# Turning HGRN's normed and gated result with VectorE's square blocks and a trip through memory instead of 16 TensorE transposes

## The chip, the cores and the metric

The kernel runs on one core of a Trainium2 chip. The metric is the device time of one execution in microseconds (us). The kernel before takes 1633.6 us, the median of 3 runs (1633.28 to 1634.9).

The core has five engines, each with its own in-order queue: TensorE (PE in the profile, its weight loads PEld), VectorE (DVE), ScalarE (ACT), GpSimd (POOL) and SyncE (SP). Here SP issues the transfers of weights, and POOL the transfers of pages through memory.

## The reference, cut to what matters

One layer works on 256 latent and 256 context tokens of 2048 features, all in float32: a modulated norm, one wide input projection, a convolution branch and a bidirectional HGRN recurrence side by side, a gated merge with an output projection, and an MLP. The change lies between the recurrence and its output projection:

```python
def hgrn_readout(o, g, norm_g, w_o):
    o = rms_norm(o, norm_g.reshape(HGRN_HEADS, HGRN_HEAD_DIM))
    o = o.reshape(o.shape[:2] + (D_HGRN,)).astype(g.dtype) * jax.nn.silu(g)
    return o @ w_o
...
y_h = hgrn_readout(o, p_g, hgrn_norm_g[l], hgrn_out_w[l])
```

There are 8 heads of 128 features. For each token and head, `o` is divided by its root mean square over the 128 features, scaled by a gain per feature and by silu of a gate per token and feature; then all 1024 features are projected to 2048.

## The kernel before

**Products.** Every float32 product is made of two-part numbers: `hi` is the value rounded to TensorE's float32r, `lo` what is left. ScalarE makes `hi` of a weight tile (`whi`, L124), VectorE makes `lo` (`wlo`, L127). A token-wise product (`tokens`, L280, through `mm3r`, L259, and `pe`, L183 and L188) does, per weight tile of 128 x 1024, four output blocks of three matmuls each: 12 matmuls of 128 x 512. A product over 16 tiles does tiles 0 to 12 one after the other, and calls `pump` after each; tiles 13 to 15 are taken together, block by block (LAST = 3), and then its four sums are evacuated. Four tiles of `hi` and `lo` are held (AHEAD = 4), five raw tiles wait or are in flight (RAWS = 5).

**Order of the work.** The Tile framework plans each engine's order when the program is built, by program order and its own estimate of when an instruction could run; an instruction that is ready may be planned far ahead of where the program has it. `issue_after` holds an instruction behind another on the same engine. Work beside the products sits in generators on the list `bg`. `pump` (L161) gives them a budget of so many us per call (1.3 here, never more than 2.5), in the order of the list, the first three only (LIVE = 3). A generator yields its cost on VectorE, or None to wait for the next call. What it issues on VectorE is held behind the last but one `wlo` (L168), so that it can't pass the weights; nothing holds what it issues on the other engines. `finish` (L177) runs a generator to its end.

**Around the change.** After the recurrence, the order of the products is: the convolution's gate and value, silu(g) (L839, tokens on partitions, kept in `self.sg`), the two merge gates (L853 and L854, each in two halves of 16 weight tiles), the HGRN output projection (`who`, L863), the convolution's projection (`wpw`). The convolution and its layer norm (`conv`, L1540) are a generator from L829 on, and the two readouts (`readout`, L1517, four heads each) follow it on the list from L841 on. They run beside the two gates, and L857 finishes them ahead of the HGRN projection.

**The readout.** Head `h` has left `o` with tokens on partitions, 2 blocks of 128 tokens by 128 features, in a page of four heads (`self.on`), and its sums of squares in `self.osq`. The readout takes the reciprocal root (L1523), multiplies by it and by silu(g) (L1528, VectorE, in place, 2 per head), turns the two blocks to features on partitions with TensorE against the identity into a PSUM bank (L1533), and evacuates it twice, scaled by the norm's gain: to `hi` by ScalarE (L1536), to `lo` by VectorE (L1537). The two parts go to `self.rp[h]`, the operand of the projection, in memory that held the context's activations.

**Pages.** On-chip buffers of 128 x 1024 floats come from one pool of 30 pages (`page`, L194); each is given back after its last reader.

**The turn without TensorE.** The MLP turns its hidden values in another way. `turn_blocks` (L1246) transposes 32 x 32 blocks of 512 columns with one VectorE instruction (L1250). `swapped` (L1279) stores the page to memory (L1284) and loads it back in four transfers (L1287) that put the blocks' rows on their partitions. `turn_hidden` (L1252) waits ten calls of `pump` and then splits the page that came back (L1270 through L240), held on ScalarE behind the newest `whi`.

Of the kernel before, what the change touches and what calls it, by code (L numbers as in the profile page):

```python
# [8 lines left out]
F32 = mybir.dt.float32  # L9
# [3 lines left out]
AF = mybir.ActivationFunctionType  # L13
ALU = mybir.AluOpType

P = 128
T = 256
# [17 lines left out]
PB = 4  # L35
# [102 lines left out]
class Kernel:  # L138
# [1378 lines left out]
    def readout(self, j):  # L1517

        nc = self.nc
        while self.ended < 4 * (j + 1):  # L1520
            yield None
        r = self.osq[:, 8 * j:8 * j + 8]
        self.rstd(r, r, 1.0 / P)  # L1523
        for h in range(4 * j, 4 * j + 4):
            o = self.at(self.on, h)
            for tb in range(2):
                s = o[:, tb * P:(tb + 1) * P]
                nc.vector.scalar_tensor_tensor(s, s, self.osq[:, 2 * h + tb:2 * h + tb + 1], self.sg[tb][:, h * P:(h + 1) * P], op0=ALU.mult, op1=ALU.mult)  # L1528
            yield 0.5
            yield None  # L1530
            ps = self.bank()
            for tb in range(2):
                nc.tensor.transpose(out=ps[:, tb * P:(tb + 1) * P], in_=o[:, tb * P:(tb + 1) * P], identity=self.v["ident"])  # L1533
            g = self.v["hng"][:, h:h + 1]
            hi, lo = self.rp[h][:, :T], self.rp[h][:, T:]
            nc.scalar.activation(out=hi, in_=ps[:, :T], func=AF.Copy, scale=g)  # L1536
            nc.vector.scalar_tensor_tensor(lo, ps[:, :T], g, hi.bitcast(F32), op0=ALU.mult, op1=ALU.subtract)  # L1537
            yield 0.5

    def conv(self, uhv, uvv):  # L1540
# [153 lines left out]
```

## Time and profile before

| | |
|---|---|
| median of 3 runs | 1633.6 us (1633.28 to 1634.9) |
| profiled execution, first to last instruction (the page gives no other time of it) | 1632.6 us |
| TensorE busy | 1615.6 us, 99% |
| VectorE busy | 1162.2 us, 71% |
| ScalarE busy | 784.3 us, 48% |
| POOL busy | 52.0 us, 3% |
| TensorE's 16 turns at L1533 | 658.3 to 711.6 us |
| evacuations of the gates, L850 | 597.7 to 739.7 us |
| bytes moved | 391.22 MB, 240 GB/s in the mean |

In the rows of the profile, `L1533 PE MATMUL bank<-pack,o` is a line of the kernel, an engine, an operation, and the tile written with the tiles read. `x16` counts instructions. A bracket such as `[0.19 <-DVE o L1528]` is the time for which the engine sat idle just before, and the instruction that ended it. Matmuls are pipelined: they are shown with their latency and overlap each other.

### The profile page before, as it was taken

The numbers are of one execution on the slowest core, as the hardware profiler recorded it, in microseconds if no ns is written. First come the engines' busy times: TensorE is split into PE (matmuls) and PEld (weight loads), VectorE is DVE, ScalarE is ACT, GpSimd is POOL, SyncE is SP. The second block draws the span as 40 slices with busy tenths as digits, with TensorE's granted clock in tenths as the row PEclk, the third lists the DMA queues.
The fourth block names the chain that finished last, engine by engine and source line by source line (L and its number), as shares of the span: only waits on it lengthen the run. The fifth ranks groups of instructions, "written<-read, shape, count | busy, mean of one in ns | idle before, by whom it ended". The sixth has DMA issues, their size and how long they took to land.

```text
span 1632.6 us, 21510 instructions
## 1 busy us (share of the span) xinstructions
PE 1615.6 (99%) x7939; PEld 1337.5 (82%) x7939; DVE 1162.2 (71%) x1686; ACT 784.3 (48%) x1094; POOL 52.0 (3%) x98
## 2 busy tenths in 40 slices
PE   7999999999999999999999999999999999999998
PEld 5668888888888888888888888888888888888887
DVE  5786887778868889977887676545665656665556
ACT  6553444434554444654446665444553455435543
POOL 0000000000000000000000001000110011001000
PEclk9999999999999999999999999999999999999999
DMA  9997954444566566787887478867887688677763
GB/s 377 402 379 281 324 175 151 149 152 135 194 202 219 182 192 205 236 279 267 320 302 254 142 259 256 287 197 235 289 283 227 217 255 284 231 240 241 232 217 114
DMA packets 109145, 391.22 MB, mean 240 GB/s; under 512 B 12912, under 2 KB 13680, under 8 KB 109040
## 3 DMA queue, kind: packets, MB, share of 16 engines
q1 hardware_dynamic: 102096, 368.60, 66.4%
q0 software_dynamic: 6656, 20.99, 4.3%
q8 instruction: 62, 1.02, 0.3%
q14 instruction: 43, 0.35, 0.1%
q10 hardware_dynamic: 288, 0.26, 0.0%
HBM read 379.32 MB, written 10.49 MB: 239 GB/s over the span
## 4 chain that ended last, share of the span: by engine, by line
PE 94%; DVE 2%; DMA 1%; issue 1%; ACT 1%; SPq 0%; ACTq 0%; DVEq 0%
PE bank L188 82%; PE bank L255 5%; PE bank L257 3%; PE bank L1465 2%; DVE wlo L127 1%; DMA x<-ctx 1%; ACT whi L124 0%; DMA raw<-who 0%; PE bank L1496 0%; PE bank L1507 0%; PE bank L1505 0%; DMA raw<-wpw 0%; DVE gacc L1301 0%; SPq L526 0%; PE bank L1360 0%
## 5 line engine op out<-in xcount | busy, mean ns | idle before, releaser
L127 DVE TENSOR_TENSOR wlo<-raw,whi 128x1024 fp32r<-128x1024 f32 x488 | 593.0, 1222 | 321.2 <-ACT whi L124 315.1
L124 ACT ACTIVATE whi<-raw 128x1024 fp32r<-128x1024 f32 x488 | 512.9, 1059 | 605.2 <-PE bank L188 388.5
L188 PE MATMUL bank<-whi,h 128*128 128x512 f32 x2160 | 674.1, 390 | 2.0 <-DVE h L673 1.2
L188 PEld LDWEIGHTS bank<-whi,h 128*128 128x128 f32 x2160 | 405.1, 188 | 88.0 <-DVE h L673 2.1
L188 PE MATMUL bank<-wlo,h 128*128 128x512 f32 x1080 | 420.7, 390 | 1.3 <-DVE wlo L127 1.3
L188 PEld LDWEIGHTS bank<-wlo,h 128*128 128x128 f32 x1080 | 202.8, 188 | 44.9 <-DVE wlo L127 3.5
L188 PE MATMUL bank<-whi,hidh 128*128 128x512 f32 x503 | 195.0, 388 | 0.0
L188 PE MATMUL bank<-wlo,hidh 128*128 128x512 f32 x503 | 195.0, 388 | 0.0
L188 PE MATMUL bank<-whi,hidl 128*128 128x512 f32 x503 | 195.0, 388 | 0.0
L188 PE MATMUL bank<-h,whi 128*128 128x512 f32 x512 | 166.2, 405 | 0.0
L188 PEld LDWEIGHTS bank<-whi,hidl 128*128 128x128 f32 x503 | 94.4, 188 | 19.5
L188 PEld LDWEIGHTS bank<-wlo,hidh 128*128 128x128 f32 x503 | 94.4, 188 | 19.3
L188 PEld LDWEIGHTS bank<-whi,hidh 128*128 128x128 f32 x503 | 94.4, 188 | 19.3
L188 PEld LDWEIGHTS bank<-h,whi 128*128 128x128 f32 x512 | 91.3, 189 | 20.6 <-issue 6.2
L188 PE MATMUL bank<-h,wlo 128*128 128x512 f32 x256 | 100.0, 391 | 0.0
L255 PE MATMUL bank<-h,whi 128*128 128x512 f32 x384 | 97.8, 396 | 0.0
L255 PEld LDWEIGHTS bank<-h,whi 128*128 128x128 f32 x384 | 69.0, 189 | 12.4
L1314 DVE SCALAR_TENSOR_TENSOR raw<-raw,silu_row 128x1024 f32<-128x1024 f32 x64 | 76.6, 1219 | 0.4 <-DMA raw<-wmt 0.3
L1301 DVE SCALAR_TENSOR_TENSOR gacc<-raw,silu_c,gacc 128x1024 f32<-128x1024 f32 x60 | 76.7, 1278 | 0.0
L188 PEld LDWEIGHTS bank<-h,wlo 128*128 128x128 f32 x256 | 48.1, 188 | 10.2
L257 PEld LDWEIGHTS bank<-h,wlo 128*128 128x128 f32 x384 | 52.4, 190 | 3.9
L257 PE MATMUL bank<-h,wlo 128*128 128x256 f32 x384 | 53.5, 282 | 0.0
(246 smaller groups left out, 1374.5 us busy)
## 6 DMA issues: line engine op xcount, KB each, us to landing
raw<-w SPq DMA_DIRECT2D x256, 512.0 KB, 4.8
raw<-wi SPq DMA_DIRECT2D x172, 512.0 KB, 4.5
raw<-wmt SPq DMA_DIRECT2D x64, 512.0 KB, 4.3
raw<-wm SPq DMA_DIRECT2D x64, 512.0 KB, 4.8
rawpage<-wm SPq DMA_DIRECT2D x42, 512.0 KB, 9.7
raw<-wo SPq DMA_DIRECT2D x32, 512.0 KB, 4.8
raw<-who SPq DMA_DIRECT2D x16, 512.0 KB, 5.1
raw<-wpw SPq DMA_DIRECT2D x16, 512.0 KB, 5.6
```

What stands on the lines that cost most here:

```text
L124: kn.his.append(nc.scalar.activation(out=hi, in_=raw, func=AF.Copy))
L127: kn.los.append(nc.vector.tensor_tensor(lo, raw, hi.bitcast(F32), op=ALU.subtract))
L188: ins = fn(*args, **kw)
L255: nc.tensor.matmul(bank, w[0][:, cut(i)], x(k)[2], start=(k == 0), stop=False)
L257: nc.tensor.matmul(bank[:, T:], w[1][:, cut(i)], x(k)[0], start=False, stop=(k == nk - 1))
L1301: nc.vector.scalar_tensor_tensor(acc, raw, s, acc, op0=ALU.mult, op1=ALU.add)
L1314: nc.vector.scalar_tensor_tensor(raw, raw, 1.0, self.srow, op0=ALU.mult, op1=ALU.mult, accum_out=self.dot[:, 32 * j + b:32 * j + b + 1])
L1465: nc.tensor.matmul(ps[:, b * P:(b + 1) * P], w, r, start=True, stop=True)
```

## The change

The readout no longer uses TensorE or PSUM. L1528 stays, and the generator yields once for two heads. When the four heads of a readout are done, VectorE transposes 32 x 32 blocks of their page into a new page, `oflip`, with two instructions of 512 columns; the page is stored to memory and loaded back in four transfers by `swapped`, into another page; the generator passes eight calls of `pump`; then, for each head, ScalarE copies the head's columns out of the returned page into a small buffer (`gained`), putting the blocks in order and scaling by the norm's gain, and `split` makes `hi` (ScalarE) and `lo` (VectorE) of it.

```diff
@@ readout
                 nc.vector.scalar_tensor_tensor(s, s, self.osq[:, 2 * h + tb:2 * h + tb + 1], self.sg[tb][:, h * P:(h + 1) * P], op0=ALU.mult, op1=ALU.mult)
-            yield 0.5
+            if h % 2:
+                yield 0.5
+        flip = self.page(F32, "oflip")
+        for n in range(2):
+            self.turn_blocks(flip, n, self.on[j][:, n * 512:(n + 1) * 512])
+            yield 0.7
+        back = self.swapped(flip).rearrange("p (i b r) -> p b i r", i=4, b=8)
+        for _ in range(8):
             yield None
-            ps = self.bank()
-            for tb in range(2):
-                nc.tensor.transpose(out=ps[:, tb * P:(tb + 1) * P], in_=o[:, tb * P:(tb + 1) * P], identity=self.v["ident"])
-            g = self.v["hng"][:, h:h + 1]
-            hi, lo = self.rp[h][:, :T], self.rp[h][:, T:]
-            nc.scalar.activation(out=hi, in_=ps[:, :T], func=AF.Copy, scale=g)
-            nc.vector.scalar_tensor_tensor(lo, ps[:, :T], g, hi.bitcast(F32), op0=ALU.mult, op1=ALU.subtract)
+        for n in range(PB):
+            h = PB * j + n
+            g, src = self.v["hng"][:, h:h + 1], back[:, 2 * n:2 * n + 2]
+            t = self.small(T, "gained")
+            nc.scalar.activation(out=t.rearrange("p (b i r) -> p b i r", b=2, i=4), in_=src, func=AF.Copy, scale=g)
+            self.split(t, self.rp[h][:, :T], self.rp[h][:, T:])
             yield 0.5
```

The helpers that it calls, unchanged:

```python
def turn_blocks(self, page, j, src):
    out = page[:, :TW].rearrange("p (j b r) -> p b j r", j=4, b=8)[:, 4 * j:4 * j + 4]
    self.nc.vector.transpose(out=out, in_=src.rearrange("p (b j r) -> p b j r", b=4, j=4))

def swapped(self, page):
    there = self.dr.tile([P, TW], F32, name="there", tag="there", bufs=4)
    nc.gpsimd.dma_start(there, page[:, :TW])
    back = self.page(F32, "back")[:, :TW]
    for j in range(4):
        nc.gpsimd.dma_start(back[32 * j:32 * j + 32].rearrange("c (i f) -> c i f", i=4),
                            there[:, j * T:(j + 1) * T].rearrange("(i c) f -> c i f", i=4))
    return back
```

## The prediction

> **What bounds the kernel now.** I read the page's first part, then the stretch in which the readouts run, then the chain of waits inside it.
>
> ```profile
> span 1632.6 us, 21510 instructions
> PE 1615.6 (99%) x7939; PEld 1337.5 (82%) x7939; DVE 1162.2 (71%) x1686; ACT 784.3 (48%) x1094; POOL 52.0 (3%) x98
> ```
>
> TensorE is busy for 99% of the span, so a turn taken off it can shorten the kernel by what the turn takes there, and by no more. The 16 turns, and the products that feed them, run between 658 and 712 us (here the instructions that touch the tile `o`, with minimum, median and maximum ns):
>
> ```profile
> L1528 DVE SCALAR_TENSOR_TENSOR o<-o,osq,silu_g x16: 339/347/352, 657.9 to 710.1; 128x128 f32<-128x128 f32 x16
> L1533 PEld LDWEIGHTS bank<-pack,o x16: 137/139/143, 658.3 to 711.5; 128*128 128x128 f32 x16
> L1533 PE MATMUL bank<-pack,o x16: 270/272/329, 658.3 to 711.6; 128*128 128x128 f32 x16
> ```
>
> Busy time by stretch; after the stretch come its length, then PE, PEld, DVE, ACT and POOL busy with counts, the clock, the DMA share and GB/s:
>
> ```profile
> 655.00:690.00 35.00, 34.81 (x157) 27.94 (x156) 35.00 (x52) 20.48 (x26) 0.00 (x0) 1.00 0.70 229
> 700.00:740.00 40.00, 40.00 (x180) 33.09 (x179) 27.33 (x34) 20.64 (x29) 1.20 (x2) 1.00 0.79 269
> ```
>
> VectorE is busy for all of 655 to 690 us: there two engines are full at once, since the convolution's layer norm runs beside the readouts. From 700 to 740 VectorE has a third to spare.
>
> **The turns on TensorE.** 272 ns is a latency; what a turn keeps from the next product is read from TensorE's order in time (start, us, engine, line, operation):
>
> ```profile
> 657.52 0.39 PE L188 MATMUL bank<-wlo,h 128*128 128x512 f32 x1
> 657.75 0.39 PE L188 MATMUL bank<-whi,h 128*128 128x512 f32 x1
> 658.33 1.12 PE L1533 MATMUL bank<-pack,o 128*128 128x128 f32 x4 [0.19 <-DVE o L1528]
> 659.20 0.48 PE L188 MATMUL bank<-whi,h 128*128 128x512 f32 x1
> 659.52 0.40 PE L188 MATMUL bank<-wlo,h 128*128 128x512 f32 x1
> ```
>
> And the chain of waits in the same run, where a pair of turns is followed by products alone:
>
> ```profile
> 681.04 0.22 PE bank L1533 x2
> 681.26 24.72 PE bank L188 x108
> ```
>
> A product takes 24.72 / 108 = 0.229 us, three of them 0.69. From one `wlo` product to the next, with the first four turns between, 2.00 us pass: 1.31 more, 0.4 of it the wait for L1528. Each of the six later pairs stands in the chain with 0.22 us. The sum is 1.31 + 6 x 0.22 = 2.6 us. [...]
>
> **What VectorE and ScalarE gain and lose.** The evacuations L1536 and L1537 go. What comes has rows of its like: the split at L240 of the same shape, and the MLP's block turn L1250 (same helper, same shape). Instructions that write or read `h`, on ScalarE and then on VectorE, and the block turn:
>
> ```profile
> L1536 ACT ACTIVATE h<-bank,pack x8: 452/458/479, 659.2 to 712.7; 128x256 fp32r<-128x256 f32 x8
> L240 ACT ACTIVATE h<-conv x8: 400/402/419, 699.1 to 708.0; 128x256 fp32r<-128x256 f32 x8
> ```
>
> ```profile
> L1537 DVE SCALAR_TENSOR_TENSOR h<-bank,pack,h x8: 390/476/482, 661.5 to 713.8; 128x256 fp32r<-128x256 f32 x8
> L240 DVE TENSOR_TENSOR h<-conv,h x8: 415/418/424, 700.1 to 709.1; 128x256 fp32r<-128x256 f32 x8
> ```
>
> ```profile
> L1250 DVE STREAM_TRANSPOSE turned<-rsq x32: 702/711/712, 968.4 to 1540.2; 128x512 f32<-128x512 f32 x32
> ```
>
> VectorE: 4 x 0.71 + 8 x 0.42 - 8 x 0.48 = +2.4 us. ScalarE: each of 8 heads gets a scaled copy and a split for one evacuation; the copy has a scattered source and no row of its own, so it lies between 0.40 (L240) and 0.61 (the MLP's split of a swapped page has twice the elements and the same scattered source; I take 0.45). That is 8 x (0.45 + 0.40 - 0.46) = +3.1 us, 2.7 to 4.4. Neither engine is full over the span, so these cost nothing by themselves, if they fall where there is room.
>
> Where they fall follows from the generators. Walked through with the credit rule of `pump` (1.3 a step, at most 2.5, first three generators), the order of before comes out as in the trace: four turns at step 4 of the second gate's first half, pairs at steps 6, 10, 10, 11, and 4 and 6 of its second half. By the same walk the new readout 0 is turned at steps 3 and 4 (about 660 to 662 us) and readout 1 at step 9 (about 677 us); the gains and splits are emitted at steps 6 and 9 of the second half (about 711 and 720 us), in the stretch with room. So up to 688 us VectorE loses 6 L1537 (2.86), and gets 4 block turns (2.84) and 2 more L1528 (0.69): **+0.7 us in the one stretch where it is full**.
>
> **What that does to TensorE.** The last three weight tiles of a half are used together, so the last `wlo` of the half is needed soonest after its slot is freed. VectorE, the weight load that waits, and ScalarE's `whi` for that tile:
>
> ```profile
> 683.13 1.75 DVE L384 RECIPROCAL lnmu<-lnmu 128x256 f32<-128x256 f32 x1
> 684.80 0.39 DVE L1537 SCALAR_TENSOR_TENSOR h<-bank,pack,h 128x256 fp32r<-128x256 f32 x1
> 685.10 2.35 DVE L1601 TENSOR_TENSOR conv<-conv,lnmu 128x1024 f32<-128x1024 f32 x2
> 687.37 1.22 DVE L127 TENSOR_TENSOR wlo<-raw,whi 128x1024 fp32r<-128x1024 f32 x1
> ```
>
> ```profile
> 688.64 0.19 PEld L188 LDWEIGHTS bank<-wlo,h 128*128 128x128 f32 x1 [0.29 <-DVE wlo L127]
> ```
>
> ```profile
> 684.06 1.06 ACT L124 ACTIVATE whi<-raw 128x1024 fp32r<-128x1024 f32 x1 [0.63 <-PE bank L188]
> ```
>
> TensorE is already late here by 0.29 us, because the two multiplies at L1601 stand ahead of `wlo`. After the change it comes here 1.31 + 4 x 0.22 = 2.2 us sooner, and VectorE is 0.7 us later. Kept in this order, `wlo` ends at 688.6 + 0.7 = 689.3, and of the saving only the two pairs after it are left: 0.7 - 0.4 = +0.3 us, nothing won. But `whi` waits only for TensorE (0.63 us in its row), so it too comes up to 2.2 us sooner, and `wlo`, emitted before the layer norm's step, may be planned ahead of L1601: ahead of one multiply -0.9 us, of both -2.0, of the reciprocal as well -2.6. I take **-1.6**, between one and both, since VectorE reaches the pair 0.7 later and `wlo` is ready 2.2 sooner. Bounds -2.6 and +0.3.
>
> **The transfers.** Each readout adds a store of 512 KB and four loads of 128 KB on POOL's queue, where before the change nothing is issued for 350 us:
>
> ```profile
> 708.36 0.62 POOL L1341 DMA_DIRECT2D bias<-bgain  x1 [349.79 <-ACT h L240]
> ```
>
> Behind a load that waits for its store stand this `bias` and L1342's `gain`, due at 708 us; SP's weights are not passed. The same five transfers in the MLP, issue to landing, and their order on POOL:
>
> ```profile
> there<-turned POOLq DMA_DIRECT2D x4, 512.0 KB, 7.3
> back<-there POOLq DMA_DIRECT2D x16, 128.0 KB, 6.7
> ```
>
> ```profile
> 970.55 0.54 POOL L1284 DMA_DIRECT2D there<-turned  x1 [157.91 <-DVE turned L1250]
> 977.11 2.21 POOL L1287 DMA_DIRECT2D back<-there  x4 [6.02 <-PE bank L188]
> 979.31 0.57 POOL L1284 DMA_DIRECT2D there<-turned  x1
> ```
>
> Store, four issues and the last load come to 0.5 + 7.3 + 2.2 + 6.7 = 16.7 us: readout 0 is back at 679 us, readout 1 at about 694. The product that reads them starts when the last gate is evacuated:
>
> ```profile
> L850 ACT ACTIVATE gate<-bank x16: 576/598/601, 597.7 to 739.7; 128x512 f32<-128x512 f32 x16
> ```
>
> That leaves readout 1 some 45 us; the round trip is hidden, and without that cover it would cost up to 16.7 us. In the MLP the down product lives beside twice these transfers with no idle time before its matmuls:
>
> ```profile
> L188 PE MATMUL bank<-whi,hidh 128*128 128x512 f32 x503 | 195.0, 388 | 0.0
> ```
>
> I charge contention with 0: at 229 GB/s for a share of 0.70, 2.1 MB are 6.4 us of all DMA engines, and 30% of 35 us, 10.5, are free; if they held weights back for all 6.4 us, the three tiles ahead (below) would leave 0.4. [...]
>
> **The sum.** 1632.6 (span) - 1.6 = 1631.0 for the span. The median of the runs, 1633.6, is 1.0 above that span, so 1632.0.
>
> **Rivals.** First, *the saving goes into the wait for `wlo`*: the order on VectorE stays, +0.3, 1633.9. For it: VectorE's 35.00 of 35.00. Against: `whi` is freed sooner. [...]
>
> Second, on the other side, *ScalarE is queued behind the returning page*. The new copies are not held to a place on ScalarE; `pump` orders only VectorE. What ScalarE may take early, it takes, as the readouts' square roots show, run as soon as the heads end though the readouts are pushed just ahead of the gates (first evacuation 597.7):
>
> ```profile
> L383 ACT ACTIVATE osq<-osq,eps x2: 300/300/301, 360.7 to 488.4; 128x8 f32<-128x8 f32 x2
> ```
>
> And the planner thinks the store short. On POOL the second store is planned behind the loads that wait for the first one, though its page is ready at 974.8 us, 4.2 us after the first store's issue at 970.55:
>
> ```profile
> 974.07 0.70 DVE L1250 STREAM_TRANSPOSE turned<-rsq 128x512 f32<-128x512 f32 x1
> ```
>
>  If the copies stand where the planner lets the page land, some 6 us early (3 for each leg), ScalarE stops at about 673 to 679 us, and behind it the next `whi`, its `wlo` and all of VectorE's queue. Three tiles ahead are 3 x 12 x 0.229 = 8.2 us, less 2.3 for `whi` and `wlo`: 6 us are covered on an idle VectorE, but this one is full, so what it idles comes out at 688 us: 6 us, less the 2.3 by which it lags behind `whi` (685.1 to 687.4), less what ScalarE makes good, 1.5 to 3.7; I take 2. With the order kept: +0.3 + 2 = +2.3, 1635.9; from a stop of 8 us on, over 1637. The same stop for readout 1 falls at 688 to 694 us, where no slot for `whi` is free anyway.
>
> Third, *more than the turns*: the new order also loses the 0.29 us at 688 and small waits near it: 1630.3. Fourth, *a page is not there*: the `bias` above got its page only at 708 us, so the pool of 30 is full until then. Counted in program order, the four new pages still fit (`on` and `silu_g` are given back early). If not, the second return would land at 708 + 2.2 + 6.7 = 717 us; ScalarE, queued behind it from about 694 with 8.2 us of tiles ready, would stop TensorE for some 12 us from where the forecast stands: 1644.
>
> **Chances.** Forecast 0.45, first rival 0.20, second 0.21, third 0.08, fourth 0.06. The likeliest case alone spans 1631.0 to 1632.8. What a measurement of this kernel can tell from no change is about 0.2%, 3.3 us. The forecast and the first rival lie within it. Faster by more needs under 1630.3: half of the third and a tail of the forecast, 0.14 in all. Slower by more needs over 1636.9: the upper part of the second, and the fourth, with some for an order that I don't foresee: 0.19. The rest is 0.67. The range of 8 in 10 runs from 1630.2 to 1637.3.
>
> **What would show it.** No L1533 and 4 L1250 more between 655 and 680 us; VectorE still full there; at the end of that half, `wlo` ahead of L1601 (forecast) or a weight load waiting about 3 us for it (first rival). On ScalarE, idle time before the copies that ends with `back` near 679 us is the second rival; copies near 711 and 720 us without a wait refute it. The forecast is wrong if TensorE's idle time between 655 and 740 us grows beyond 2 us, or if stages that the change doesn't touch move.

## The result

The changed kernel takes 1636.55 us (median of 18 runs, 1633.81 to 1639.05), the kernel before beside it on the same chip 1633.88 us (18 runs, 1632.21 to 1634.9). The ratio is 1.0018, with a 95% interval of 1.0012 to 1.0025: slower by 0.18%, where the prediction had it faster by 0.1%. The time lies in the predicted range (1630.2 to 1637.3), on the wrong side of the kernel before.

### The profile after

The head of the profile's page of the changed kernel, and its busy time by stretch (columns as in the prediction: length, PE, PEld, DVE, ACT, POOL with counts, clock, DMA share, GB/s):

```profile
span 1635.7 us, 21506 instructions
PE 1615.5 (99%) x7923; PEld 1336.6 (82%) x7923; DVE 1164.3 (71%) x1690; ACT 786.4 (48%) x1102; POOL 57.9 (4%) x108
```

```profile
655.00:690.00 35.00, 33.29 (x147) 27.24 (x146) 31.44 (x48) 16.89 (x23) 5.93 (x10) 1.00 0.87 264
690.00:700.00 10.00, 7.21 (x31) 5.42 (x30) 6.01 (x6) 9.30 (x14) 0.00 (x0) 1.00 0.60 223
700.00:740.00 40.00, 40.00 (x171) 32.94 (x170) 30.55 (x40) 23.89 (x40) 1.10 (x2) 0.96 0.85 289
```

The 16 turns are gone (7939 matmuls before, 7923 after), and yet TensorE is as busy as before, 1615.5 us, and the span is 3.1 us longer. Two things show. Between 655 and 700 us TensorE now stands still for 1.7 + 2.8 us, where it was idle for 0.2 us before. And from 700 to 740 us its granted clock is 0.96: as many microseconds are busy, but 0.04 x 40 = 1.6 of them are lost to a slower clock. The DMA share of the first stretch has risen from 0.70 to 0.87, and VectorE, full there before, is busy for only 31.44 us of 35.

TensorE's order in time in the changed kernel has three stops (start, us, engine, line, operation, and in the bracket the idle time before it and what ended it); the last row is one of the products after them, at half clock, 0.63 us where 0.39 is usual:

```profile
678.76 0.50 PE L188 MATMUL bank<-wlo,h 128*128 128x512 f32 x1 [1.71 <-DVE wlo L127]
...
698.11 0.50 PE L188 MATMUL bank<-whi,h 128*128 128x512 f32 x1 [2.04 <-ACT whi L124]
699.37 0.50 PE L188 MATMUL bank<-wlo,h 128*128 128x512 f32 x1 [0.76 <-DVE wlo L127]
...
700.26 0.63 PE L188 MATMUL bank<-wlo,h 128*128 128x512 f32 x1
```

**The first stop** comes from VectorE. Its rows in time, same kernel:

```profile
671.75 0.71 DVE L1250 STREAM_TRANSPOSE oflip<-o 128x512 f32<-128x512 f32 x1
...
673.68 3.90 DVE L1575 TENSOR_REDUCE lnred<-lnsq 128x256 f32<-128x1024 f32 x2
677.48 2.36 DVE L127 TENSOR_TENSOR wlo<-raw,whi 128x1024 fp32r<-128x1024 f32 x2
```

The fourth block turn, one `wlo`, the layer norm's two reduces, 3.90 us, and only then the `wlo` that TensorE waits for since 677.05. The reduces stood ahead of the same `wlo` (the 156th of the program) before, and TensorE did not wait:

```profile
674.09 2.01 DVE L1569 TENSOR_REDUCE lnred<-lnsq 128x256 f32<-128x1024 f32 x1
676.01 1.22 DVE L127 TENSOR_TENSOR wlo<-raw,whi 128x1024 fp32r<-128x1024 f32 x1
```

So the order at this place is the old one, but VectorE comes to it 1.5 us later (677.48 in place of 676.01): ahead of it lie now all four block turns and all 16 of L1528, of which 10 lay ahead before. And TensorE, without the turns, comes sooner.

At 688 us, where the prediction looked for the wait, the order has changed. The `wlo` (the 160th) that stood behind the reciprocal and both multiplies now stands ahead of all three, and TensorE doesn't wait for it:

```profile
683.72 1.23 DVE L127 TENSOR_TENSOR wlo<-raw,whi 128x1024 fp32r<-128x1024 f32 x1 [0.86 <-ACT whi L124]
...
688.85 1.74 DVE L384 RECIPROCAL lnmu<-lnmu 128x256 f32<-128x256 f32 x1
...
692.78 2.35 DVE L1607 TENSOR_TENSOR conv<-conv,lnmu 128x1024 f32<-128x1024 f32 x2
```

**The second and third stop** follow from a weight that came late. The chain of waits of the changed kernel, and ScalarE's split of that weight (the bracket is ScalarE's own wait):

```profile
680.54 9.91 DMA raw<-wi
```

```profile
690.55 1.06 ACT L124 ACTIVATE whi<-raw 128x1024 fp32r<-128x1024 f32 x1 [5.07 <-DMA raw<-wi]
```

A weight page issued at 680.54 lands 9.91 us later. It is no single case. The DMA issues between 680 and 692 us, with count, size and median us from issue to landing, first after, then before:

```profile
raw<-wi SPq DMA_DIRECT2D x4, 512.0 KB, 10.1
raw<-wm SPq DMA_DIRECT2D x2, 512.0 KB, 9.2
back<-there POOLq DMA_DIRECT2D x4, 128.0 KB, 8.2
```

```profile
raw<-wi SPq DMA_DIRECT2D x5, 512.0 KB, 5.0
raw<-wm SPq DMA_DIRECT2D x1, 512.0 KB, 4.9
```

Beside the four loads of the second returning page the weights take twice their time. ScalarE, which works in order, stands idle for 5.07 us behind the late weight. From 691.5 to 697.0 us it then does what has gathered (a scaled copy, a table load, evacuations of the gate, steps of the layer norm), and only after that the next `whi`, for which TensorE waits from 696.07 us on.

**The returning page** holds ScalarE up for little:

```profile
674.72 0.91 ACT L1542 ACTIVATE gained<-back,pack 128x256 f32<-128x256 f32 x2 [1.23 <-DMA back<-there]
```

So there were three theories of the loss to tell apart. **A**: the trips through memory crowd the weights' loads. **B**: VectorE is too full, or in the wrong order, where the block turns meet the layer norm. **C**: the scaled copies stand too early on ScalarE and hold up `whi` (the prediction's second rival).

### The profile page after: what moved, and what is told of

Read it like the earlier page. It is cut to its first block, busy times and chain, and to the rows that moved or that the text cites. A ratio compares the mean times of both kernels' runs of the same rounds, so it can differ in the third digit from the quotient of the medians.

```text
span 1635.7 us, 21506 instructions
## 1 busy us (share of the span) xinstructions
PE 1615.5 (99%) x7923; PEld 1336.6 (82%) x7923; DVE 1164.3 (71%) x1690; ACT 786.4 (48%) x1102; POOL 57.9 (4%) x108
## 4 chain that ended last, share of the span: by engine, by line
PE 90%; DMA 4%; DVE 4%; ACT 1%; issue 1%; SPq 0%; ACTq 0%; DVEq 0%
PE bank L188 78%; PE bank L255 5%; PE bank L257 3%; PE bank L1465 2%; DMA raw<-wi 2%; DVE wlo L127 1%; DMA rawpage<-wms 1%; DMA x<-ctx 1%; ACT whi L124 1%; DMA raw<-wpw 0%; PE bank L1496 0%; PE bank L1507 0%; PE bank L1505 0%; DVE lnred L1575 0%; DVE o L1528 0%
```

## The experiments

The kernel before was run beside each group of kernels on the same chip: 1633.59 us (33 runs) beside the first four below, 1633.27 us (21) beside the control of the order and the last kernel, 1633.28 us (31) beside the others; each kernel has 9 to 11 runs. Spans of single profiled executions vary by some 2 us between kernels of equal median (1630.3 and 1632.6 us for the control of the order and the kernel before), so times are compared by medians, and the traces are read for where a stop stands.

### Without the trips

```diff
-        back = self.swapped(flip).rearrange("p (i b r) -> p b i r", i=4, b=8)
+        back = flip[:, :TW].rearrange("p (i b r) -> p b i r", i=4, b=8)
```

> The kernel after, with the store to memory and the four loads of each readout left out: the copies read the page that VectorE turned, so the result isn't the reference's. VectorE, ScalarE and TensorE have the same work as in the kernel after (1636.6 us). Theory A (the trips crowd the weights: raw tiles land after 10 us in place of 5, and everything behind them is late): the stops of TensorE at 698 and 699 us go, and with them the 3.4 us at half clock; 1631 to 1633 us. Theory B (VectorE is too full from 655 to 690 us, the trips only happen to fall there): the stops stay, 1635 to 1637. Theory C (ScalarE stands behind the returning page, 1.2 us in the trace of after): 1635 to 1636.

Measured: 1632.48 us, ratio 0.9994 (0.9985 to 1.0003). TensorE's only stop in this stretch, and the weights' landing between 680 and 692 us:

```profile
679.63 0.50 PE L188 MATMUL bank<-wlo,h 128*128 128x512 f32 x1 [1.70 <-DVE wlo L127]
```

```profile
raw<-wi SPq DMA_DIRECT2D x5, 512.0 KB, 5.3
```

The stops near 698 us are gone with the trips, the weights land in 5.3 us again, and the stop near 679 us stays as it was. Against the changed kernel, each by its own kernel before, this is 3.8 us less (1.1 under before in place of 2.7 over it).

### The trips alone

The kernel before with all its turns on TensorE; beside them a page is stored and loaded back, once for each readout.

```diff
@@ readout, kernel before
+            if h == (1, 6)[j]:
+                nc.vector.tensor_copy(self.sg[j][:, 0:1], self.sg[j][:, 0:1])
+                self.swapped(self.sg[j])
```

> The kernel before, with TensorE's turns, and beside them a store and four loads for each readout at the places where the kernel after has them (the page of silu(g) goes out and comes back, and nobody reads it; one VectorE copy of 128 x 1 each sets the time). Theory A: slower than before by what after loses, 1.7 us and more beyond the turns: 1636 to 1640. Theory B and theory C: 1633 to 1635, since VectorE's and ScalarE's work is that of before.

Measured: 1637.04 us, ratio 1.0021 (1.0012 to 1.003), 3.4 us over the kernel before. TensorE's stops, ScalarE's order ahead of them, and the landings between 680 and 692 us:

```profile
698.09 0.50 PE L188 MATMUL bank<-whi,h 128*128 128x512 f32 x1 [0.62 <-ACT whi L124]
699.35 0.50 PE L188 MATMUL bank<-wlo,h 128*128 128x512 f32 x1 [0.76 <-DVE wlo L127]
```

```profile
696.49 0.60 ACT L850 ACTIVATE gate<-bank 128x512 f32<-128x512 f32 x1 [3.52 <-DMA back<-there]
696.99 1.99 ACT L124 ACTIVATE whi<-raw 128x1024 fp32r<-128x1024 f32 x2
```

```profile
raw<-wi SPq DMA_DIRECT2D x4, 512.0 KB, 7.1
```

The weights land in 7.1 us. But the 1.4 us of stops near 698 us have another cause here than in the change: an evacuation of the gate waits 3.52 us for the four loads of the returning page, and the `whi` that TensorE needs is queued behind it. A likely reason is that nobody reads this page, so that its buffer is given to the gate as soon as the loads are through; in the trace of the change no evacuation waits for `back`. The second trip also starts 8 us later than in the change (its store at 680.46 us, not 672.75). So this run shows that a trip beside these products is not free, but not how much of the 3.4 us is the crowding of the weights. Its stops do not add up to 3.4 us either; the runs of this kernel spread from 1634.5 to 1639.3 us, and one trace is one of them.

### The copies held on ScalarE

```diff
-            nc.scalar.activation(out=t.rearrange("p (b i r) -> p b i r", b=2, i=4), in_=src, func=AF.Copy, scale=g)
-            self.split(t, self.rp[h][:, :T], self.rp[h][:, T:])
+            with self.tc.issue_after(self.his[-1].ins):
+                nc.scalar.activation(out=t.rearrange("p (b i r) -> p b i r", b=2, i=4), in_=src, func=AF.Copy, scale=g)
+                self.split(t, self.rp[h][:, :T], self.rp[h][:, T:])
```

> The kernel after, with the copies and splits on ScalarE held behind the newest whi, as the MLP's are, so that they can't be queued ahead of their place in the program. Theory C: the wait for the page goes and no whi stands behind it, 1633 to 1635. Theories A and B: as after, 1635.5 to 1637.5.

Measured: 1635.07 us, ratio 1.0011 (1.0002 to 1.002). The interval overlaps that of the change. TensorE's first two stops stand where they stood:

```profile
678.44 0.50 PE L188 MATMUL bank<-wlo,h 128*128 128x512 f32 x1 [1.68 <-DVE wlo L127]
697.38 0.50 PE L188 MATMUL bank<-whi,h 128*128 128x512 f32 x1 [1.63 <-ACT whi L124]
```

Theory C falls as the main cause: with the copies out of the way of `whi`, both stops are there. Whether holding them is worth the 1.2 us between the medians (1.5 over the kernel before in place of 2.7), these runs can't say.

### The turns taken away, and nothing put in their place

```diff
@@ readout, kernel before
-            ps = self.bank()
-            for tb in range(2):
-                nc.tensor.transpose(out=ps[:, tb * P:(tb + 1) * P], in_=o[:, tb * P:(tb + 1) * P], identity=self.v["ident"])
+            ps = o
```

> The kernel before, with TensorE's 16 turns left out and nothing in their place: the two evacuations read the unturned page, so the result isn't the reference's. This is what the turns are worth on TensorE. By the sum in the prediction 2.6 us, so 1631.3; if VectorE's last wlo of the half then holds TensorE (no work is added to it here), 1632 to 1633; by 0.39 us a turn 1627.6.

Measured: 1634.55 us, ratio 1.0007 (0.9999 to 1.0016). 2.6 us of TensorE's work are left out, and the kernel doesn't gain. One stop, and VectorE's order ahead of it:

```profile
689.15 0.79 PE L188 MATMUL bank<-wlo,h 128*128 128x512 f32 x1 [3.07 <-DVE wlo L127]
```

```profile
683.81 1.75 DVE L384 RECIPROCAL lnmu<-lnmu 128x256 f32<-128x256 f32 x1 [0.56 <-ACT lnmu L383]
685.60 2.36 DVE L1599 TENSOR_TENSOR conv<-conv,lnmu 128x1024 f32<-128x1024 f32 x2
687.88 1.22 DVE L127 TENSOR_TENSOR wlo<-raw,whi 128x1024 fp32r<-128x1024 f32 x1
```

For this kernel it is the prediction's first rival to the letter: the reciprocal and both multiplies (L1601 in the kernel before) keep their place ahead of `wlo`, and TensorE, which comes sooner, waits 3.07 us for it. The clock falls with it, by stretch in the same kernel:

```profile
655.00:690.00 35.00, 31.93 (x140) 26.15 (x139) 34.41 (x51) 20.57 (x26) 0.00 (x0) 0.97 0.66 230
690.00:700.00 10.00, 10.00 (x35) 7.93 (x35) 3.40 (x4) 7.56 (x13) 0.00 (x0) 0.76 0.46 159
```

The low clock takes 0.03 x 35 + 0.24 x 10 = 3.4 us off these stretches, some 0.5 of it while TensorE stood still anyway. This execution is the slowest of the eleven (1636.82 us). In five of them the mean granted clock is 0.999, and they take 1633.0 to 1634.5 us; in the other six it is 0.997 or 0.998. So part of the median is this fall of the clock.

### The same, with `wlo` put ahead of the layer norm

```diff
@@ conv, beside the edit above
-        self.rstd(m[:, :T], mu, 1.0)
+        yield None
+        with self.tc.issue_after(self.los[-1].ins):
+            self.rstd(m[:, :T], mu, 1.0)
```

> The kernel before without its 16 turns on TensorE (the evacuations read the unturned page, so the turn is left out of the computation), as in the run named no_turn (1634.55 us, with a stop of 3.07 us behind the reciprocal and two multiplies of the layer norm), and with the layer norm's reciprocal held behind the last wlo that has been emitted. Theory B (the turns' 2.6 us are there, and VectorE's order eats them): the stop near 689 us shrinks below 1 us and the time is 1630.5 to 1631.5 us. If the turns are worth nothing on TensorE, or the wait comes from elsewhere, it stays at 1633.5 to 1635 us.

Measured: 1631.82 us, ratio 0.999 (0.9982 to 0.9999): 2.4 us less than with the old order, each by its own kernel before, and 1.5 less than the kernel before. The turns' time is there to be won, and in the run before this one VectorE's order had eaten it. The expected 1630.5 to 1631.5 was missed by 0.3 us: two stops of 0.23 and 0.77 us remain near 685 us. The control is the kernel before with the second edit alone:

> The kernel before, turns and all, with only the layer norm's reciprocal held behind the last wlo, as in the run named no_turn_wlo_first (1631.82 us). What it can win is the stop of 0.29 us near 688 us: 1633.0 to 1633.6 us, if the 1.5 us that no_turn_wlo_first lies under the kernel before come from the turns that it leaves out. If they come from the order by itself, 1631.5 to 1632.3 us.

Measured: 1633.3 us, ratio 0.9998 (0.9989 to 1.0007). The order by itself wins nothing; the gain comes from the turns.

### The block turns alone

```diff
@@ readout, kernel before
+            if h == (1, 6)[j]:
+                flip = self.page(F32, "oflip")
+                for n in range(2):
+                    self.turn_blocks(flip, n, self.sg[j][:, n * 512:(n + 1) * 512])
```

> The kernel before, with its 16 turns on TensorE, and four block turns of a page beside them that nobody reads: VectorE's share of the change without any transfer. Theory B (VectorE too full): the 2.84 us come out at the last weight tile of the half that ends near 688 us, a stop of 2 to 3 us in place of 0.29 us: 1635.5 to 1636.5 us. Theory A (only the trips cost): no change beyond 0.5 us, 1633.4 to 1634.2 us, and the weights' landing stays at 5 us.

Measured: 1635.35 us, ratio 1.0015 (1.0006 to 1.0024), 2.1 us over the kernel before. TensorE's stop and VectorE's rows ahead of it:

```profile
690.16 0.50 PE L188 MATMUL bank<-wlo,h 128*128 128x512 f32 x1 [1.43 <-DVE wlo L127]
```

```profile
681.21 1.29 DVE L1250 STREAM_TRANSPOSE oflip<-silu_g 128x512 f32<-128x512 f32 x2
...
688.90 1.21 DVE L127 TENSOR_TENSOR wlo<-raw,whi 128x1024 fp32r<-128x1024 f32 x1
```

2.84 us more on a full VectorE cost 2.1 us, with no transfer in it. The stop stands near 690 us, where the order of before has it, and not near 679 us as in the change. Theory B is no alternative to A: the block turns cost time without a trip, and the change loses 3.8 us less without its trips. The time lies just under what B expected and well over what A did.

### The readouts later

The change with the copies held, and the readouts begun only when the convolution is done.

```diff
-        conv = self.push(self.conv(uhv, uvv))
+        conv = self.after = self.push(self.conv(uhv, uvv))
...
-        while self.ended < 4 * (j + 1):
+        while self.ended < 4 * (j + 1) or self.after in self.bg:
```

> The readouts wait until the convolution is done, so that the block turns and trips run at some 705 to 735 us, after the layer norm, where VectorE has a third to spare and the DMA engines have a share of 0.79 already without the trips; the copies are held as in the run named held (1635.07 us). Theory A (the trips crowd the weights): the stop moves with the trips; weights issued at 705 to 735 us land in 8 to 10 us in place of 5, and TensorE stops for 2 us or more there: 1635 to 1638 us. Theory B (VectorE too full): no stop at 679 us, none at 698 us, 1631.0 to 1632.5 us.

Measured: 1637.45 us, ratio 1.0026 (1.0016 to 1.0036). VectorE is no longer full (30.32 us of the 35 from 655, 28.12 of the 40 from 700), and yet it is no faster than the change: by the medians 1.5 us slower, though the intervals overlap. Issues between 712 and 740 us, TensorE's longest stop, and the stretch:

```profile
raw<-wm SPq DMA_DIRECT2D x4, 512.0 KB, 8.2
raw<-wi SPq DMA_DIRECT2D x4, 512.0 KB, 9.3
```

```profile
732.20 0.79 PE L188 MATMUL bank<-whi,h 128*128 128x512 f32 x1 [1.78 <-ACT whi L124]
```

```profile
700.00:740.00 40.00, 36.60 (x144) 28.20 (x143) 28.12 (x45) 15.74 (x22) 6.70 (x12) 0.91 0.89 286
```

As theory A expected, the long landings went where the trips went, and the stop with them. It is not the late weights alone: ahead of the `whi` of this stop ScalarE also does four of the scaled copies and their splits (728.27 to 731.10 us). TensorE is idle for 3.4 us there, and the clock takes 0.09 x 40 = 3.6 us off the stretch, some 0.5 of it while TensorE stood still anyway.

### The readouts sooner

The change with the copies held, and the readouts put ahead of the convolution in the list, so that they run beside the first gate's products and the layer norm comes later.

```diff
-        for j in range(2):
-            heads.append(self.push(self.readout(j)))
+        for j in (1, 0):
+            gen = self.readout(j)
+            self.bg.appendleft(gen)
+            heads.append(gen)
```

> The readouts stand ahead of the convolution in the list, so that the block turns, the trips through memory and the scaled copies run some 60 to 100 us sooner, where the DMA engines have a smaller share (0.60 to 0.66 against 0.70 to 0.79), and the layer norm runs after them; the copies are held behind ScalarE's last weight split, as in the run named held (1635.07 us). Theory A (the trips crowd the weights): the weights of the gate land in 5 to 6 us at 680 to 692 us, the stop of 2.4 us near 698 us goes, and the time is 1632.0 to 1632.8 us; where the trips now run, the weights' landing grows. Theory B (VectorE is too full where the turns and the layer norm meet): the stop of 1.7 us near 679 us goes as well, since the two no longer meet: 1631.0 to 1632.0 us. If a trip costs 2 to 3 us of TensorE wherever it runs, 1634.5 to 1636.5 us.

Measured: 1632.24 us, ratio 0.9994 (0.9986 to 1.0003). The same trips now cost nothing that can be seen: no stop near 698 us, and no stop from 560 to 640 us, though beside the trip the weights land later there too. Issues between 580 and 590 us, then TensorE's one stop and VectorE's rows ahead of it:

```profile
raw<-wi SPq DMA_DIRECT2D x5, 512.0 KB, 5.2
back<-there POOLq DMA_DIRECT2D x4, 128.0 KB, 6.6
```

```profile
676.99 0.50 PE L188 MATMUL bank<-wlo,h 128*128 128x512 f32 x1 [1.65 <-DVE wlo L127]
```

```profile
673.92 1.89 DVE lnred L1578
675.81 1.14 DVE wlo L127
```

(The last two rows are of the chain of waits: start, us, engine, tile, line.) Theory A held. Theory B's part did not: the stop near 677 us stayed, since the layer norm moved along, and now its first two reduces (at 648 to 654 us in the change) stand ahead of `wlo` there. Why the trip is harmless here has a likely reason in the issues of the kernel before, from 560 to 610 us and from 655 to 740 us:

```profile
raw<-wi SPq DMA_DIRECT2D x19, 512.0 KB, 4.3
```

```profile
raw<-wi SPq DMA_DIRECT2D x24, 512.0 KB, 4.7
raw<-wm SPq DMA_DIRECT2D x9, 512.0 KB, 4.6
raw<-who SPq DMA_DIRECT2D x4, 512.0 KB, 4.8
raw<-wmt SPq DMA_DIRECT2D x1, 512.0 KB, 5.1
```

That is one page of weights in 50 / 19 = 2.6 us, and later one in 85 / 38 = 2.2 us, since other weights come between the `wi`. That leaves more room early on. That this is the reason is argued, not shown.

### The readouts sooner, and the reduces apart

```diff
@@ conv, beside the edit above
-        red = sums(y)
-        yield 2.4
-        yield None
+        red = self.small(512, "lnred")
+        for j in range(2):
+            with self.tc.issue_after(self.los[-1 if j else -2].ins):
+                nc.vector.tensor_reduce(red[:, j * T:(j + 1) * T], kt_(y[j]).rearrange("p b t -> p t b"), axis=mybir.AxisListType.X, op=ALU.add)
+            yield 1.2
+            yield None
```

> The run named early (1632.24 us; one stop left, 1.65 us near 677 us, where the two reduces of the layer norm stand ahead of three wlo) with the second reduce held behind the last wlo that has been emitted, so that two wlo stand between the reduces. Theory B (the order on VectorE): the stop near 677 us shrinks below 0.5 us and nothing of the 2.6 us of the turns is eaten: 1630.2 to 1631.2 us, faster than the kernel before by 0.12 to 0.2%. If the stop only moves to the next wait for wlo (the second half of the layer norm, near 688 us): 1631.8 to 1632.8 us.

Measured: 1631.25 us, ratio 0.9986 (0.9977 to 0.9995). It is faster than the kernel before, by 2.0 us, and than the change, and just above what was expected of theory B. TensorE's one wait from 640 to 760 us, and VectorE's order:

```profile
674.17 0.50 PE L188 MATMUL bank<-wlo,h 128*128 128x512 f32 x1 [0.20 <-DVE wlo L127]
```

```profile
670.85 2.03 DVE L1589 TENSOR_REDUCE lnred<-conv 128x256 f32<-128x1024 f32 x1
...
672.90 2.35 DVE L127 TENSOR_TENSOR wlo<-raw,whi 128x1024 fp32r<-128x1024 f32 x2
```

With two `wlo` between the reduces the stop is 0.20 us. With the copies held and the order mended, the change is worth something; its first place cost more than it won.

## Why the prediction was wrong

**What the turns are worth** (1.31 + 6 x 0.22 = 2.6 us) is borne out as far as the medians reach: 1.5 us came out when the turns were left out and `wlo` had its way, with 1.0 us of stops still in that trace, and 2.0 us in the last kernel, with 0.20 us of stops. No run shows the 0.39 us a turn behind the lowest time that was expected with the turns taken away (1627.6); in the chain of the kernel before a pair of turns stands with 0.22 us, 0.11 a turn.

**What VectorE and ScalarE get** was sized nearly rightly. The block turns take 704 to 710 ns (forecast 0.71), the scaled copy 493 ns at the median (0.45 taken, 0.40 to 0.61 allowed). Readout 0 was turned at 658.8 and 661.6 us (forecast about 660 to 662), readout 1 at 666.6 and 671.7 (about 677, so up to 10 us early). All this work thereby came to lie ahead of the reduces at 673.7 us, where VectorE was late by 1.5 us, while "+0.7 us" was a sum up to 688 us; and the second trip came to lie beside the weights of 680 to 692 us.

**"I charge contention with 0" is the step that failed.** The change without its trips is 3.8 us faster and comes to 1.1 us under the kernel before, where the sum had 1.6; this term alone turned the forecast's gain into a loss. The sum of bytes (6.4 us of all DMA engines, 10.5 free) was an average over 35 us, and "the three tiles ahead would leave 0.4" took the delay as one push. The trip did not keep to the gaps: the weights issued beside the returning page land in 9 to 10 us at the median in place of 5, for several tiles in a row. Why the free time elsewhere in the stretch did not help is not shown by any run. That the MLP lives with twice these transfers said nothing of this place: the same trips went with weights that landed in 8.2 to 9.3 us and a time of 1637.45 us in one place (readouts later), and with 5.2 us and 1632.24 us in another (readouts sooner).

**"Ahead of one multiply -0.9, of both -2.0 ... I take -1.6" failed in its working too,** and that 1.1 us came out without the trips is luck: it is about the turns' 2.6 less a stop of 1.7 that the sum didn't have. The sign that the prediction named, `wlo` ahead of L1601, is there in the changed kernel (683.72 against 692.78 us), even ahead of the reciprocal. But TensorE's wait had moved 10 us earlier, to the `wlo` behind the two reduces (1.71 us), a place that the prediction did not look at. Nor did the shorter work on TensorE bring the new order about: with the turns gone and nothing else changed, the order at 688 us was the old one and the wait 3.07 us, as in the first rival. What made the planner change it in the changed kernel stays open. The rival's price, +0.3, left out what follows a stop (below).

**The second rival** had nearly the right time (1635.9) for another reason. ScalarE waited for the returning page for 1.23 us, not 6, and with the copies held the stops remained. **The fourth** did not occur: the pages were there, and the second trip's loads were issued at 679.75 us. **The third** can't be told from the forecast by these runs.

By the trace the span grew by 3.1 us: 2.6 saved, 4.5 of stops and 1.6 of slower clock come to +3.5, which is within what single executions differ by.

## What to carry to other kernels

When a saving on the bottleneck moves work to other engines, look at the instruction that hands the bottleneck its next operand, and count what stands ahead of it in that engine's queue: a sooner bottleneck waits there unless the order is changed with it. Price an added transfer by how late the loads beside it will land, tile by tile, and not by the free share of the stretch; the same transfer cost 3.8 us in one place and nothing that shows 90 us sooner. A probe that adds work which nobody reads can bring waits of its own, as the trips alone did: read its trace before taking its time for a price. If a change loses, move it before giving it up: here place and order took the medians from 2.7 us over the kernel before to 2.0 us under it.

## What was not expected of the hardware

A stop of TensorE can cost more than its own length: in the change 1.6 us of slower clock come on top of the stops. In three traces the granted clock falls to half at a stop, and it does so in steps: it is low from 700.06 to 703.47 us in the change (3.41 us), from 688.06 to 694.89 with the turns taken away and from 731.67 to 738.50 with the readouts later (twice 3.41). In the trace of the change the fall comes 689.49 us after the first full clock on record (10.57 us into the span), which is 202 steps of 3.413 us; in that of the kernel before the clock is full for 1614.50 us, from 13.68 to 1628.18 us, which is 473 such steps. The first four rows are steps of 3.41 us, counted back from the fall in the same trace; the last four are single stops in traces where the clock was 1.00 all around the stop, so that nothing shows the steps there:

| kernel | step or stop, us | TensorE idle in it, us | granted clock after it |
|---|---|---|---|
| the change | 696.65 to 700.06 | 2.21 | 0.50 |
| readouts later | 728.26 to 731.67 | 2.18 | 0.50 |
| turns taken away | 684.65 to 688.06 | 1.98 | 0.50 |
| the change, first stop | 676.17 to 679.58 | 1.71 | 1.00 |
| without the trips | 677.93 to 679.63 | 1.70 | 1.00 |
| readouts sooner | 675.34 to 676.99 | 1.65 | 1.00 |
| copies held | 695.75 to 697.38 | 1.63 | 1.00 |
| block turns alone | 688.73 to 690.16 | 1.43 | 1.00 |

In the four steps the clock was half after 1.98 us of idle time and more (1.98 of the stop of 3.07 with the turns taken away; 1.45 of the stop of 2.04, and the 0.76, in the change), and whole after 1.71. None of the four stops of 1.43 to 1.70 us was followed by a low clock, nor was the stop of 0.76 us that comes next with the copies held (it ends at 698.64 us). That the idle time within one step decides would fit this, but it is an estimate from eight cases, each from one execution, and not shown.

This goes with the wider spread of the changed kernel's runs (5.2 us, against 2.7 before). In 8 of the 18 the mean granted clock is 0.997 or 0.998, and they take 1636.5 to 1639.05 us; in the other 10 it is 0.999 or 1.000, and they take 1633.8 to 1637.2. In the 85 runs of the kernel before beside the experiments it is never under 0.999. Where in those runs the clock fell is not shown.
